# A two-layer hybrid attention and recurrent block on one core: operand splits moved to the projection, softmax scale moved behind the product, two more buffers in the mixer, three weights split ahead

## Chip, cores and metric

One core of one Trainium2 chip runs the whole program in one launch. The metric is the device time of an execution in microseconds (us), lower is better. Engines: TensorE (PE; PEld is its weight load), VectorE (DVE), ScalarE (ACT), GpSimd (POOL), and SyncE (SP), which issues all DMAs of this kernel.

## What is computed

Two layers over 1024 latent tokens and 256 context tokens of width 1024, all in float32. Only the parts around the change are shown.

```python
# layer 0: 4 differential heads (two 64-wide maps each) and 8 neighbourhood heads
w  = softmax(q0 k0) - lam * softmax(q1 k1)              # diff_attend
oa = head_rms_norm(w @ v, subln_g) * (1 - lambda_init)
s  = concat(s_loc + bias, s_ctx); p = softmax(s)        # neighbourhood_attend
ob = p_loc @ v_loc + p_ctx @ v_ctx
out = concat(oa, ob) @ w_out
# layer 1: Griffin block; both directions d, then
out = ((r_fwd + r_bwd) * gelu(y)) @ w_out
# after each mixer and each ConvFFN: x <- LN(alpha * x + gate * F(mod(x)))
```

## The kernel before, in words

**Precision.** A float32 operand of a large product is split into two fp32r tiles: `h`, a cast of the raw value, and `l = raw - h`. `split` (L101 to L103) makes the cast on ACT and the difference on DVE unless another engine is named; `weight` (L117) loads a raw weight into a ring of three (`wr`), and splits it into a ring of six (`wq`), with the difference on POOL by default. `mm3` (L122) then runs three products. In attention the split is stacked: `qs` holds `h` of a 64-wide query in partitions 0 to 63 and `l` in 64 to 127, and `kh`, `kl` hold the key's `h` and `l` in both halves.

**Order.** Each engine executes its instructions in one order. A planner lays the program out by its own costs; where `in_turn` (L91) chains instructions under a key (`att_pe`, `att_dve`, `att_act`, `att_pool`, `rnn`, `rnn_dve`), their written order is kept. SP issues loads and stores in one queue, and one that waits holds those behind it.

**Query and key projection** (`qkv`, L436 to L476). Sixteen blocks `n`, each 8 x 3 x 3 products into three PSUM chunks (banks 4, 6, 7 in rotation), copied with a scale by ACT into `q` (L463, one buffer). For the first eight blocks a rotary step follows: shuffle and two operations on DVE (L468, L469, L471), the cosine product on POOL (L470). `q` is stored to `qk_s`. Between chunks, one step of `ada` (L205) is taken: it reduces rows of the modulation weights, two DVE operations per 512 KB weight, 48 steps in all; its raw weights share the ring `wr`.

**Heads** (`heads`, L479). For each head and each half `m`, `qk_s` is loaded twice into both partition halves of `qr` and `kr`; DVE copies (L500, L503) and POOL subtracts (L501, L505; for the first head L507 on DVE) make `qs`, `kh`, `kl`. It is a generator, stepped while the head before is computed (`ahead`, L1303 and L1418).

**Attention** (`attention`, L537). 36 differential units (4 heads x (8 query blocks + context)), then 68 neighbourhood units (4 head pairs x (8 blocks x 2 heads + context)). A unit makes scores, a maximum on DVE (L1327; L1449 and L1450), an exponential on ACT, transposes on PE (L523), copies to SBUF on ACT, and the product with `v`. In a neighbourhood unit the probabilities are scaled by the reciprocal sum on DVE (L1469) before the transposes; the product has `v` (64 columns) as weights and 128 query columns streaming (L1505), so its result is already transposed and goes to `o` (L1507), stored once per pair (L1497).

**Output projection** (`proj_ln`, L680). Weight `w[k]` is loaded and split at its step `k` (L727); the planner places these.

**Recurrent mixer** (`rnn`, L1089). Eight blocks. Gate values live in lanes 0 to 3 (`lane`, L1122): lanes 0 and 1 alternate between two places from block to block, lanes 2 and 3 have one. The two scan results, in lanes 2 and 3, are added on POOL (L1178) and multiplied on DVE (L1179); all ACT functions are chained under `rnn`.

Of the kernel before, what the change touches and what calls it, by code (L numbers as in the profile page):

```python
# [57 lines left out]
class Kernel:  # L58
    def __init__(self, nc, tc, es, a):
# [4 lines left out]
        self.cast = None  # L64
        self.const = self.pool(es, "const", 1)
# [3 lines left out]
        self.qk_s = [d.tile([P, T], F32, name=f"qk_s{i}", tag=f"qk_s{i}") for i in range(16)]  # L69
# [283 lines left out]
    def qkv(self, esa):  # L353
        nc, a = self.nc, self.a
        with ExitStack() as es:
# [80 lines left out]
            with ExitStack() as es1:  # L436
# [9 lines left out]
                for n, i in enumerate((0, 4, 1, 5, 2, 6, 3, 7, 8, 12, 9, 13, 10, 14, 11, 15)):  # L446
                    w = self.weight(a["w_qk"][i])
# [10 lines left out]
                    q = qp.tile([P, T], F32, name="q", tag="q")  # L458
# [20 lines left out]
    def heads(self, n, out, sub=None):  # L479

        nc = self.nc
# [5 lines left out]
        for m in range(2):  # L487

            rows = slice(m * 64, m * 64 + 64)
            qr = pool.tile([P, T], F32, name="qr", tag="qr")  # L490
            kr = pool.tile([P, T], F32, name="kr", tag="kr")
            for t_, i in ((qr, iq), (kr, ik)):
                self.ld(t_[0:64], self.qk_s[i][rows])
                self.ld(t_[64:128], self.qk_s[i][rows])
# [4 lines left out]
            yield  # L499
            self.dve(nc.vector.tensor_copy(qs, qr))  # L500
            self.pl(nc.gpsimd.tensor_sub(qs[64:128], qr[64:128], qs[64:128].bitcast(F32)))  # L501
            yield
            self.dve(nc.vector.tensor_copy(kh, kr))  # L503
            if sub is None:
                self.pl(nc.gpsimd.tensor_sub(kl, kr, kh.bitcast(F32)))  # L505
            else:
                sub.tensor_sub(kl, kr, kh.bitcast(F32))  # L507
# [29 lines left out]
    def attention(self):  # L537
# [3 lines left out]
        with ExitStack() as es:  # L541
# [8 lines left out]
            due = []  # L550
# [36 lines left out]
            for i in range(nd, len(units) + 2):  # L587
# [92 lines left out]
    def proj_ln(self, src, w, nk, l, which, nt, x_in, x_out, nx, fold, sizes, more=(), held={},  # L680
# [8 lines left out]
        with ExitStack() as es:  # L689
# [14 lines left out]
            for size in sizes:  # L704
# [11 lines left out]
                for k in range(nk):  # L716
# [10 lines left out]
                    wh, wl = self.weight(w[k], (P, D), nc.vector)  # L727
# [361 lines left out]
    def rnn(self, left):  # L1089
# [32 lines left out]
        def lane(i, n):  # L1122

            j = {0: 0, 1: 1, 4: 2}.get(i)
            if j is not None and n % 2:
# [11 lines left out]
        def gates(n, g, xs, x, yg):  # L1137
# [39 lines left out]
            if n < KD - 1:  # L1177
                nc.gpsimd.tensor_add(ro, ro, sx[1][:, :TL])  # L1178
# [116 lines left out]
class DiffAttention:  # L1295
    def __init__(self, kn):
        self.kn = kn
        self.heads, self.outs = [], {}
        for _ in kn.heads(0, self.heads, kn.nc.vector):
            pass  # L1300
# [87 lines left out]
class NatAttention:  # L1388
# [3 lines left out]
    def __init__(self, kn, heads):  # L1392
# [4 lines left out]
        self.slot, self.pair = 0, 4  # L1397
        self.first = self.tables(0)
# [32 lines left out]
    def unit(self, pr, j, m):  # L1431
# [35 lines left out]
        for u in range(nu):  # L1467
            sl = slice(u * n // nu, (u + 1) * n // nu)
            kn.dve(nc.vector.tensor_scalar_mul(p[:, sl], p[:, sl], rr[:, u:u + 1]))  # L1469
# [8 lines left out]
        if j < NTL and nr == 9:  # L1478
            kn.turn(bb[:64, 2 * P:3 * P], p[:, 8 * GW:9 * GW])
        yield  # L1480
        for pt, g0, gn, c0 in work:
            kn.act(pT[:, g0 * P:(g0 + gn) * P], pt[:, :gn * P], AF.Copy)
        if j < NTL and nr == 9:
            kn.dve(nc.vector.tensor_copy(pT[:64, 6 * P:7 * P], bb[:64, 2 * P:3 * P]))
        yield
        if pr not in self.outs:
            self.outs[pr] = pool.tile([P, T], F32, name="o", tag="o", bufs=2)
        o = self.outs[pr]
        if j == NTL:
            for u in range(4):  # L1490
                hs, qs = slice(u % 2 * 64, u % 2 * 64 + 64), slice(u // 2 * P, u // 2 * P + P)
                for k in range(2):
                    kn.mm(ba[hs, qs], v[:, NTL + k, hs], pT[:, (2 * u + k) * P:(2 * u + k + 1) * P],
                          start=k == 0, stop=k == 1)
            yield
            kn.act(o[:, TL:], ba[:, :TC], AF.Copy)
            kn.st(kn.att_s[4 + pr], o)  # L1497
# [4 lines left out]
        hs = slice(m * 64, m * 64 + 64)  # L1502
        po = bb[hs, 3 * P:]
# [103 lines left out]
```

## Time and profile before

| what | value |
|---|---|
| median of the 3 runs shown | 3009.2 us (3004.59 to 3010.11) |
| the profiled execution's own time | 3005.08 us |
| its span, first to last instruction | 3003.3 us |
| PE / DVE / ACT / POOL busy | 95% / 69% / 49% / 31% of the span |
| granted TensorE clock, mean | 0.982 of full speed |

The span is the first to the last instruction; a busy share is an average over stages with different limits, so the stages have to be read one by one. A line of the trace names engine, source line, tiles (output <- inputs) and shapes; an idle time is put down to the instruction that released it.

### The profile page before, as it was taken

The page shows a single profiled execution, that of the slowest core. Times are in us where ns is not written, and L with a number is a line of the kernel's source. Part 1 is how long each engine was busy: PE and PEld are TensorE (multiplying, and loading weights), DVE is VectorE, ACT ScalarE, POOL GpSimd, SP SyncE. Part 2 cuts the span into 40 slices and gives each one's busy share as a digit, 9 for nine tenths or more (in the row PEclk, how much of TensorE's full clock was granted, in tenths as well). Part 3 has the DMA queues.
Part 4 walks back from the last instruction along what each step waited for, and adds up shares of the span by engine and source line. Part 5 has one row for each costly group of instructions (what it writes and reads, how often), then busy time and mean ns, then how long its engine had stood idle before and what let it go on. Part 6 is the DMA issues. An engine that isn't in the chain of part 4 may idle for free. (4 is left out here: it accounts for less than half of the span.)

```text
span 3003.3 us, 38303 instructions
## 1 busy us (share of the span) xinstructions
PE 2859.1 (95%) x14430; PEld 2367.8 (79%) x14430; DVE 2061.9 (69%) x2743; ACT 1475.3 (49%) x2358; POOL 931.3 (31%) x636
## 2 busy tenths in 40 slices
PE   8987988889999999999999999999989999999998
PEld 5876777778887888778888888777767888888876
DVE  6079759988866787875556645566688977777364
ACT  4211136666666664344444434466767554454232
POOL 4134204543300015354430000244311366761001
PEclk9998999999999999999999999999989999999999
DMA  6365542223208413632126646311146122225452
GB/s 227 128 183 194 198 158 71 71 62 87 61 29 279 175 63 107 189 119 69 69 77 215 217 158 206 100 49 50 51 164 232 64 84 79 80 77 201 146 196 99
DMA packets 133596, 381.60 MB, mean 127 GB/s; under 512 B 14334, under 2 KB 39966, under 8 KB 133282
## 3 DMA queue, kind: packets, MB, share of 16 engines
q1 hardware_dynamic: 133410, 379.15, 38.2%
q8 instruction: 113, 1.85, 0.3%
q14 instruction: 73, 0.60, 0.1%
HBM read 310.13 MB, written 68.97 MB: 126 GB/s over the span
## 5 line engine op out<-in xcount | busy, mean ns | idle before, releaser
L124 PE MATMUL pb<-wl,a 128*128 128x512 f32 x1040 | 397.6, 393 | 2.7 <-DVE wl L103 2.7
L125 PE MATMUL pb<-wh,a 128*128 128x512 f32 x1040 | 394.8, 392 | 0.8 <-DVE a L103 0.7
L123 PE MATMUL pb<-wh,a 128*128 128x512 f32 x1040 | 387.5, 393 | 7.0 <-ACT a L102 5.1
L102 ACT CAST wh<-wr 128x1024 fp32r<-128x1024 f32 x182 | 191.3, 1051 | 407.3 <-PE pb L124 282.3
L103 DVE TENSOR_TENSOR wl<-wr,wh 128x1024 fp32r<-128x1024 f32 x166 | 202.8, 1223 | 234.5 <-ACT wh L102 233.3
L123 PE MATMUL pb<-hh,wh 128*128 128x512 f32 (+1 forms) x704 | 263.8, 375 | 31.7 <-ACT q L463 31.0
L124 PE MATMUL pb<-hl,wh 128*128 128x512 f32 (+1 forms) x704 | 261.7, 372 | 1.3 <-DVE hl L669 1.3
L125 PE MATMUL pb<-hh,wl 128*128 128x512 f32 (+1 forms) x704 | 261.4, 371 | 0.0
L646 POOL TENSOR_SCALAR s<-s 128x1 f32<-128x1 f32 x36 | 16.0, 446 | 769.6 <-ACT x L645 768.9
L123 PEld LDWEIGHTS pb<-wh,a 128*128 128x128 f32 x1040 | 195.4, 188 | 50.8 <-ACT a L102 6.5
L124 PEld LDWEIGHTS pb<-wl,a 128*128 128x128 f32 x1040 | 195.3, 188 | 44.2 <-DVE wl L103 4.2
L125 PEld LDWEIGHTS pb<-wh,a 128*128 128x128 f32 x1040 | 195.3, 188 | 42.2 <-DVE a L103 2.1
L103 POOL TENSOR_TENSOR wq<-sq,wq 128x512 fp32r<-128x512 f32 x96 | 157.0, 1639 | 193.8 <-ACT wq L102 193.0
L517 ACT ACTIVATE p<-pb,nm 128x1280 f32<-128x1280 f32 (+3 forms) x160 | 158.8, 995 | 67.6 <-DVE nm L1327 65.9
L896 POOL TENSOR_TENSOR sq<-wr 128x512 f32<-128x512 f32 x72 | 120.2, 1669 | 225.4 <-DMA wr<-w_up 216.3
L123 PEld LDWEIGHTS pb<-hh,wh 128*128 128x128 f32 x704 | 137.3, 195 | 55.0 <-ACT q L463 32.7
L852 DVE SCALAR_TENSOR_TENSOR lane<-lane,cv 128x1023 f32<-128x1023 f32 x88 | 128.2, 1459 | 52.2 <-ACT lane L851 51.9
L123 PE MATMUL pb<-t,wq 128*128 128x512 f32 x400 | 157.6, 395 | 4.9 <-DVE lane L1031 4.5
L124 PE MATMUL pb<-t,wq 128*128 128x512 f32 x400 | 157.9, 395 | 0.0
L125 PE MATMUL pb<-t,wq 128*128 128x512 f32 x400 | 157.8, 395 | 0.0
L124 PEld LDWEIGHTS pb<-hl,wh 128*128 128x128 f32 x704 | 137.3, 195 | 23.8 <-DVE hl L669 1.5
L125 PEld LDWEIGHTS pb<-hh,wl 128*128 128x128 f32 x704 | 136.8, 194 | 22.6
(323 smaller groups left out, 7598.0 us busy)
## 6 DMA issues: line engine op xcount, KB each, us to landing
wr<-w_dn SPq DMA_DIRECT2D x110, 512.0 KB, 3.6
wr<-w_up SPq DMA_DIRECT2D x88, 512.0 KB, 3.6
wr<-ada_w SPq DMA_DIRECT2D x80, 512.0 KB, 3.9
ar<-g_s SPq DMA_DIRECT2D x88, 256.0 KB, 3.7
wr<-w_ao SPq DMA_DIRECT2D x32, 512.0 KB, 5.4
g_s<-lane SPq DMA_DIRECT2D x22, 640.0 KB, 3.0
x_s<-y SPq DMA_DIRECT2D x26, 512.0 KB, 6.0
x<-x_s SPq DMA_DIRECT2D x26, 512.0 KB, 5.5
```

What stands on the lines that cost most here:

```text
L102: self.cast = self.nc.scalar.copy(h, raw)
L103: (sub or self.nc.vector).tensor_sub(l, raw, h.bitcast(F32))
L123: i = mm(out, a[0], b[0], start=first, stop=False, **kw)
L124: mm(out, a[0], b[1], start=False, stop=False, **kw)
L125: j = mm(out, a[1], b[0], start=False, stop=last, **kw)
L517: self.in_turn("att_act", self.nc.scalar.activation(*args, **kw))
L646: nc.gpsimd.tensor_scalar(rs, sq, 1.0 / D, EPS, op0=ALU.mult, op1=ALU.add)
L852: nc.vector.scalar_tensor_tensor(c[:, 1:], u[:, :n - 1], cvw[:, 0:1], c[:, 1:], op0=ALU.mult, op1=ALU.add)
L896: op(have[n], x, y)
```

## The change

Seven edits.

1. In the q/k projection the weight's difference goes from POOL to DVE, and the rotary cosine product too. `q` gets a second buffer. Each block is then split: a cast `h` on ACT, `l` on DVE in place of `q`, and both are stored (two stores for one).
2. `heads` loads `h` and `l` straight into `qs`, `kh`, `kl`: six loads per half for four, no DVE and no POOL work.
3. A neighbourhood unit no longer scales its probabilities (L1469 goes). Its product takes the transposed probabilities as weights (128 columns) and streams 64 columns of `v`; the reciprocal sum becomes the scale of ACT's copy to `o`.
4. `o` is therefore untransposed: 40 blocks of 128 x 128 are turned on PE and copied by ACT, one at a time with later units (`turned`), the rest at the end (`finish`).
5. `weight_ahead`: the first three weights of the output projection are loaded and split in the attention's own order, in the last five units.
6. In the mixer lanes 2 and 3 of odd blocks get tiles of their own.
7. The sum of the two scans goes from POOL to DVE (blocks 0 to 6).

```diff
-        self.qk_s = [d.tile([P, T], F32, name=f"qk_s{i}", tag=f"qk_s{i}") for i in range(16)]
+        self.qk_s = [d.tile([2, P, T], F32, name=f"qk_s{i}", tag=f"qk_s{i}") for i in range(16)]
...
-                    w = self.weight(a["w_qk"][i])
+                    w = self.weight(a["w_qk"][i], sub=nc.vector)
...
-                    q = qp.tile([P, T], F32, name="q", tag="q")
+                    q = qp.tile([P, T], F32, name="q", tag="q", bufs=2)
+                    h = qp.tile([P, T], F32R, name="qh", tag="qh")
...
-                        nc.gpsimd.tensor_mul(q[:, :TL], q[:, :TL], cos)
+                        nc.vector.tensor_mul(q[:, :TL], q[:, :TL], cos)
                         nc.vector.tensor_add(q[:, :TL], q[:, :TL], rot)
-                    self.st(self.qk_s[i], q)
+                    self.split(q, h, q.bitcast(F32R))
+                    self.st(self.qk_s[i][0], h.bitcast(F32))
+                    self.st(self.qk_s[i][1], q)
...
-            qr = pool.tile([P, T], F32, name="qr", tag="qr")
-            kr = pool.tile([P, T], F32, name="kr", tag="kr")
-            for t_, i in ((qr, iq), (kr, ik)):
-                self.ld(t_[0:64], self.qk_s[i][rows])
-                self.ld(t_[64:128], self.qk_s[i][rows])
...
-            self.dve(nc.vector.tensor_copy(qs, qr))
-            self.pl(nc.gpsimd.tensor_sub(qs[64:128], qr[64:128], qs[64:128].bitcast(F32)))
...
+            for half in range(2):
+                to = slice(half * 64, half * 64 + 64)
+                self.ld(qs[to].bitcast(F32), self.qk_s[iq][half, rows])
+                self.ld(kh[to].bitcast(F32), self.qk_s[ik][0, rows])
+                self.ld(kl[to].bitcast(F32), self.qk_s[ik][1, rows])
+                yield
...
+                if 0 <= i - len(units) + 5 < 3:
+                    self.weight_ahead(i - len(units) + 5)
...
+            n.finish()
+    def weight_ahead(self, k):
+        raw = self.ring.tile([P, D], F32, name="wr", tag="wr", bufs=3)
+        h, l = (self.ring.tile([P, D], F32R, name="w" + i, tag="wq", bufs=6) for i in "hl")
+        self.ld(raw, self.a["w_ao"][k])
+        self.act(h, raw, AF.Copy)
+        self.dve(self.nc.vector.tensor_sub(l, raw, h.bitcast(F32)))
+        self.ahead[k] = h, l
...
-                    wh, wl = self.weight(w[k], (P, D), nc.vector)
+                    wh, wl = self.ahead.pop(k, None) or self.weight(w[k], (P, D), nc.vector)
...
-            if j is not None and n % 2:
+            if j is None and n % 2:
+                return big(f"lane{i}")
+            if n % 2:
...
-                nc.gpsimd.tensor_add(ro, ro, sx[1][:, :TL])
+                nc.vector.tensor_add(ro, ro, sx[1][:, :TL])
...
-            kn.dve(nc.vector.tensor_scalar_mul(p[:, sl], p[:, sl], rr[:, u:u + 1]))
...
+        out = self.turned(bb, self.unit_no) if j < NTL else None
+        self.unit_no += 1
...
+        if out:
+            out()
...
-        po = bb[hs, 3 * P:]
+        po = ba[:, :GW]
         for k, (s, n, tb) in enumerate(seq):
-            kn.mm(po, v[:n, tb, hs], pT[:n, s * P:(s + 1) * P], start=k == 0, stop=k == len(seq) - 1)
+            kn.mm(po, pT[:n, s * P:(s + 1) * P], v[:n, tb, hs], start=k == 0, stop=k == len(seq) - 1)
         yield
-        kn.act(o[hs, j * P:(j + 1) * P], po, AF.Copy)
+        kn.act(o[:, j, hs], po, AF.Copy, scale=rr)
+        if m == 1:
+            self.due.append((self.unit_no, pr, j))
+    def turned(self, bank, now):
+        if self.before or not self.due or self.due[0][0] > now:
+            return None
+        kn, (_, pr, t) = self.kn, self.due.pop(0)
+        kn.turn(bank[:, 3 * P:], self.outs[pr][:, t])
+        if t == 0:
+            self.st = self.pool.tile([P, T], F32, name="st", tag="st", bufs=1)
+        def move():
+            kn.act(self.st[:, t * P:(t + 1) * P], bank[:, 3 * P:], AF.Copy)
+            if t == NT - 1:
+                kn.st(kn.att_s[4 + pr], self.st)
+        return move
+    def finish(self):
+        bank = itertools.cycle((6, 7))
+        while self.due:
+            self.turned(self.kn.banks(next(bank)), self.unit_no)()
```

The context unit of a pair changes in the same way (four products of 64 columns each, four scaled copies).

## Rows read from the trace of the kernel before

**Rows 1.** Busy time by stage: stretch in us from the span's start, its length, then busy us of each engine with the number of instructions, granted TensorE clock, DMA share, GB/s. The stretches are: q/k projection; differential attention; neighbourhood attention; recurrent mixer.

```profile
155.00:425.00 270.00, 235.50 (x1162) 199.68 (x1162) 200.22 (x243) 46.23 (x72) 75.75 (x24) 0.94 0.55 177
425.00:690.00 265.00, 230.39 (x1588) 204.57 (x1586) 239.50 (x330) 173.06 (x381) 120.66 (x138) 0.97 0.30 86
690.00:905.00 215.00, 211.81 (x1591) 179.52 (x1590) 160.15 (x406) 138.59 (x341) 53.71 (x35) 1.00 0.22 64
...
1925.00:2190.00 265.00, 248.69 (x1176) 204.85 (x1174) 169.90 (x166) 177.49 (x160) 101.03 (x40) 0.97 0.16 51
```

**Rows 2.** The same view for the two parts of the q/k projection.

```profile
164.00:300.00 136.00, 109.32 (x528) 92.17 (x527) 128.06 (x145) 20.52 (x34) 57.81 (x18) 0.91 0.62 191
300.00:425.00 125.00, 117.18 (x591) 99.79 (x590) 72.15 (x99) 22.54 (x37) 17.93 (x7) 0.97 0.48 160
```

**Rows 3.** Who waited for whom in 155 to 425 us: total us, times, longest us.

```profile
PE pb L123 <- ACT q L463: 31.0, 8, 6.8
...
ACT q L463 <- DMA qk_s<-q: 84.1, 10, 16.3
...
SPq L83 <- DVE wr L205: 148.1, 41, 13.0
```

**Rows 4.** Groups of instructions in 155 to 425 us: line, engine, operation, shapes, count, then busy us and mean ns of one, then idle before.

```profile
L205 DVE SCALAR_TENSOR_TENSOR pb<-wr,c_rows 128x1024 f32<-128x1024 f32 x48 | 78.5, 1636 | 108.5 <-ACT c_rows L192 90.9 <-DMA wr<-ada_w 17.5
L205 DVE SCALAR_TENSOR_TENSOR wr<-wr,c_rows 128x1024 f32<-128x1024 f32 x48 | 67.1, 1399 | 1.6 <-issue 0.4
...
L468 DVE STREAM_SHUFFLE rot<-q 128x1024 f32<-128x1024 f32 x8 | 11.0, 1370 | 0.0
...
L103 POOL TENSOR_TENSOR wl<-wr,wh 128x1024 fp32r<-128x1024 f32 x14 | 42.0, 3002 | 100.5 <-ACT wh L102 94.5 <-DVE pb L205 3.4 <-PE pb L125 2.6
L470 POOL TENSOR_TENSOR q<-q,cos 128x1024 f32<-128x1024 f32 x8 | 26.3, 3289 | 86.3 <-DVE rot L468 86.3
```

**Rows 5.** Single lines in the same stretch: count, shortest, median and longest duration in ns, first and last start in us.

```profile
L205 DVE SCALAR_TENSOR_TENSOR pb<-wr,c_rows x48: 1221/1230/3978, 164.7 to 421.7; 128x1024 f32<-128x1024 f32 x48
...
L469 DVE TENSOR_TENSOR rot<-rot,sin x8: 1214/3386/3404, 171.6 to 298.7; 128x1024 f32<-128x1024 f32 x8
```

**Rows 6.** DVE in order of time in one differential head (485 to 545 us): start us, duration us.

```profile
491.56 0.22 DVE L1339 SCALAR_TENSOR_TENSOR cf<-ss,nlam,rr 128x1 f32<-128x1 f32 x1
...
508.97 0.22 DVE L1339 SCALAR_TENSOR_TENSOR cf<-ss,nlam,rr 128x1 f32<-128x1 f32 x1
...
515.96 2.91 DVE L1339 SCALAR_TENSOR_TENSOR cf<-ss,nlam,rr 128x1 f32<-128x1 f32 x1
...
539.52 0.22 DVE L1339 SCALAR_TENSOR_TENSOR cf<-ss,nlam,rr 128x1 f32<-128x1 f32 x1
```

**Rows 7.** Groups in 425 to 690 us, columns as in rows 4.

```profile
L500 DVE CAST qs<-qr 128x1280 fp32r<-128x1280 f32 x9 | 7.3, 816 | 0.0
...
L505 POOL TENSOR_TENSOR kl<-kr,kh 128x1280 fp32r<-128x1280 f32 x9 | 26.3, 2918 | 17.3 <-DVE rr L1338 15.8 <-DVE kh L503 1.5
```

**Rows 8.** All engines in order of time around 436 us; in brackets the idle time before and its releaser.

```profile
436.36 1.04 ACT L102 CAST wh<-wr 128x1024 fp32r<-128x1024 f32 x1 [5.30 <-DMA wr<-w_ao]
...
437.96 4.13 PE L520 MATMUL pb<-v,wT 128*128 128x128 f32 x20 [4.87 <-ACT wT L517]
```

**Rows 9.** Groups in 690 to 905 us, columns as in rows 4.

```profile
L1469 DVE TENSOR_SCALAR p<-p,rr 128x832 f32<-128x832 f32 x29 | 27.9, 962 | 1.0
...
L517 ACT ACTIVATE o<-pb 64x128 f32<-64x128 f32 x60 | 16.3, 272 | 59.1 <-PE pb L520 59.0
...
L520 PE MATMUL pb<-wT,v 128*64 128x128 f32 x772 | 94.2, 277 | 2.2 <-DVE wT L1484 2.2
```

**Rows 10.** PE alone in order of time in the neighbourhood stage: start us, time from the first start to the last end. A float32 product is two instructions; `128*64` is the weights' shape, `128x128` the streaming operand's.

```profile
765.60 0.40 PE L520 MATMUL pb<-kl,qs 128*128 128x512 f32 x1
765.83 0.28 PE L520 MATMUL pb<-kh,qs 128*128 128x256 f32 x1
765.95 0.28 PE L520 MATMUL pb<-kl,qs 128*128 128x256 f32 x1
766.07 0.92 PE L523 MATMUL pb<-ident,p 128*128 128x128 f32 x7
766.92 1.88 PE L520 MATMUL pb<-wT,v 128*64 128x128 f32 x14
```

**Rows 11.** The same view in a differential unit: weights of 128 columns.

```profile
563.52 2.40 PE L520 MATMUL pb<-v,wT 128*128 128x128 f32 x20
```

**Rows 12.** PE in order of time at 14 us: a product that streams only 2 columns against weights of 128 columns (5 partitions), columns as in rows 10.

```profile
13.81 1.05 PE L232 MATMUL pb<-sel,ada_rows 5*128 5x2 f32 x8 [0.66 <-ACT ada_rows L229]
```

**Rows 13.** Who waited for whom in the mixer, 1900 to 2190 us, columns as in rows 3.

```profile
PE pb L123 <- ACT lane L1120: 13.0, 6, 2.7
...
ACT lane L1120 <- DVE lane L1179: 25.4, 6, 4.8
```

**Rows 14.** All engines in order of time in one block of the mixer, as in rows 8.

```profile
2056.46 2.40 POOL L1178 TENSOR_TENSOR lane<-lane 128x1024 f32<-128x1024 f32 x1 [5.70 <-DVE lane L1174]
...
2060.22 1.33 ACT L1120 ACTIVATE lane<-pb,cv 128x1280 f32<-128x1280 f32 x1 [4.74 <-DVE lane L1179]
2061.60 0.50 PE L123 MATMUL pb<-xh,wg 128*128 128x512 f32 x1 [2.67 <-ACT lane L1120]
```

**Rows 15.** The issue of the modulation weights' loads: KB each, median us from issue to landing.

```profile
wr<-ada_w SPq DMA_DIRECT2D x80, 512.0 KB, 3.9
```

More of the change, by code (lines that the diff above doesn't have):

```diff
@@ L64, in __init__ @@
         self.cast = None
+        self.ahead = {}
         self.const = self.pool(es, "const", 1)
@@ L476, in qkv, with heads @@
             self.fold(0, 0, 0, 0, 3, 4)
-    def heads(self, n, out, sub=None):
-        nc = self.nc
+    def heads(self, n, out):
         pool = self.sets[n % 2]
@@ L549, in attention @@
             steps = [self.first] + [o.unit(*u) for o, *u in units[1:]]
-            due = []
+            due = n.before = []
             def s(i, n=1):
@@ L1298, in __init__ @@
         self.heads, self.outs = [], {}
-        for _ in kn.heads(0, self.heads, kn.nc.vector):
+        for _ in kn.heads(0, self.heads):
             pass
@@ L1397, in __init__ @@
         self.slot, self.pair = 0, 4
+        self.due, self.unit_no, self.st = [], 0, None
         self.first = self.tables(0)
@@ L1466, in unit @@
         kn.dve(nc.vector.reciprocal(rr, ss))
-        for u in range(nu):
-            sl = slice(u * n // nu, (u + 1) * n // nu)
-            kn.dve(nc.vector.tensor_scalar_mul(p[:, sl], p[:, sl], rr[:, u:u + 1]))
         yield
@@ L1486, in unit @@
         if pr not in self.outs:
-            self.outs[pr] = pool.tile([P, T], F32, name="o", tag="o", bufs=2)
+            self.outs[pr] = pool.tile([P, NT, P], F32, name="o", tag="o", bufs=2)
         o = self.outs[pr]
@@ L1490, in unit @@
             for u in range(4):
-                hs, qs = slice(u % 2 * 64, u % 2 * 64 + 64), slice(u // 2 * P, u // 2 * P + P)
                 for k in range(2):
-                    kn.mm(ba[hs, qs], v[:, NTL + k, hs], pT[:, (2 * u + k) * P:(2 * u + k + 1) * P],
-                          start=k == 0, stop=k == 1)
+                    kn.mm(ba[:, u * GW:(u + 1) * GW], pT[:, (2 * u + k) * P:(2 * u + k + 1) * P],
+                          v[:, NTL + k, u % 2 * GW:(u % 2 + 1) * GW], start=k == 0, stop=k == 1)
             yield
-            kn.act(o[:, TL:], ba[:, :TC], AF.Copy)
-            kn.st(kn.att_s[4 + pr], o)
+            for u in range(4):
+                kn.act(o[:, NTL + u // 2, u % 2 * GW:(u % 2 + 1) * GW], ba[:, u * GW:(u + 1) * GW],
+                       AF.Copy, scale=rr[:, u:u + 1])
+            self.due += [(self.unit_no, pr, t) for t in range(NTL, NT)]
             return
@@ L1501, in unit @@
             seq.append((6, 64, r0 // 2 + 4))
-        hs = slice(m * 64, m * 64 + 64)
-        po = bb[hs, 3 * P:]
+        hs = slice(m * GW, m * GW + GW)
+        po = ba[:, :GW]
         for k, (s, n, tb) in enumerate(seq):
-            kn.mm(po, v[:n, tb, hs], pT[:n, s * P:(s + 1) * P], start=k == 0, stop=k == len(seq) - 1)
+            kn.mm(po, pT[:n, s * P:(s + 1) * P], v[:n, tb, hs], start=k == 0, stop=k == len(seq) - 1)
         yield
-        kn.act(o[hs, j * P:(j + 1) * P], po, AF.Copy)
+        kn.act(o[:, j, hs], po, AF.Copy, scale=rr)
[17 more added lines that the diff above has]
+            self.turned(self.kn.banks(next(bank)), self.unit_no)()
 def _blocks(w, n):
```

7 lines of the change are left out of this document (removed).

## The prediction

> **What bounds the kernel now.** I read the busy time by stage first [rows 1]. TensorE does the work that sets the end: it is busy 235.5 of 270 us in the q/k projection, 230.4 of 265 in the differential attention, 211.8 of 215 in the neighbourhood attention and 248.7 of 265 in the mixer. So three of the four stages that the change touches have TensorE idle time to win (34.5, 34.6 and 16.3 us), and the neighbourhood stage has 3.2. In the first two the granted clock is 0.94 and 0.97, so there are also stretches at 1.2 GHz in place of 2.4, after TensorE has stood still.
>
> Second, the waits, to see who keeps TensorE waiting. In the q/k projection it waits 31.0 us for the scaled copy L463, and that copy waits 84.1 us for the store of the one buffer `q`; SP's loads wait 148.1 us for VectorE's modulation steps [rows 3]. VectorE is 94% busy in the first part (128.1 of 136 us), and 58% in the second [rows 2]. Third, VectorE's groups, against the shortest duration of the same instruction: L205 takes 1.64 us on average and 1.22 at its shortest, L469 2.58 (its median 3.39) and 1.21 [rows 4, 5]. The long ones are as long as the GpSimd operations of 3.0 and 3.3 us beside them [rows 4]: VectorE is held while GpSimd reads. The same appears in the differential units: L1339, a column of one element, takes 0.22 us, and 2.91 while GpSimd makes `kl` (2.92 us) [rows 6, 7].
>
> **Part 1, q/k projection.** Removed from GpSimd: 16 weight differences of 3.00 us and 8 cosine products of 3.29. Added on VectorE: the same 24 at 1.21 us (the shortest L469, same shape), and 16 differences of 1280 columns at 1.21 x 1.25 = 1.5 us. Removed there: the first head's copies. Nothing of this stage is left on GpSimd, so every VectorE operation goes at its shortest. A block with a rotary step and three modulation steps then costs VectorE 3 x 2 x 1.22 = 7.3, and 0.7 for reading the sums, plus shuffle 1.37 and three products or sums 3.6, plus 1.2 and 1.5: 15.7 us. Today such blocks follow each other in (298.7 - 171.6) / 7 = 18.2 us (first and last start of L469) [rows 5]. At the same 94% of VectorE they take 16.7: -10 us over 7 intervals. The eight blocks without a rotary step need 10.7 us of VectorE; TensorE needs 24 x (0.23 + 0.23 + 0.12) = 13.9 us for a block [rows 10]. They take (425 - 299) / 8 = 15.8 us today; with two `q` buffers the copy no longer waits for a store one block old. I take 14.3 for them, since the new ACT cast and the store of the single `qh` are still in line: -12 us. Sum of the part: **-22 us**. Covers: 16 casts of 1.3 us are 21 us more on ACT, which is busy 46 of 270 us; without that cover they would delay L463. Sixteen more stores of 640 KB stand in SP's queue, whose waits for VectorE get shorter; with DMA at 0.55 of its time [rows 1] there is room, and if there were none, the next thing late would be the modulation weights. Bounds: -45 (all of TensorE's idle time and the clock) and +18 (VectorE's added 3.9 us in eight blocks with nothing won, less the 13 us of the first head's copies).
>
> Here a rule speaks against the change. The Trainium skill, Perfetto Trace Analysis, Optimizing Scalar/DVE Operations, says that with a saturated VectorE some work may be moved off to ScalarE or even GpSimd, and warns that the two share an SBUF read port, so that it may not help. The first half by itself forbids this move in a stretch with VectorE at 94%, and would give +18 in place of -22; the rows side with the warning.
>
> **Part 2, heads.** Four differential heads each prepare the next head in four of their units. Units without that work follow in (508.97 - 491.56) / 3 = 5.80 us, the four with it in (539.52 - 508.97) / 4 = 7.64 [rows 6]. The difference holds a copy of 0.81 us [rows 7] and one blocked operation. Both go; loads into `qs`, `kh`, `kl` (6 per half for 4) stand in SP's queue after the release of the head before last, with DMA at 0.30. 4 x 4 x 1.84 = **-29 us**. TensorE's 34.6 us of idle time and the clock bound it at -37; copies alone, 16 x 0.81, at -13. In the neighbourhood stage the same removal is worth nothing, since TensorE is 98% busy there. If the cover of the loads were gone, the next head's scores would be late.
>
> **Part 3, weights ahead.** One load of an output weight was placed at the start of the attention: ACT sat 5.30 us before its cast, and TensorE 4.87 before the next product [rows 8]. In the attention's order this cast cannot stand there: **-5 us** (bounds -6 and 0). The three casts and differences now stand among the last units, where ACT waits 59 us for TensorE [rows 9]: nothing; if a weight landed late, the exponentials behind the cast would be late.
>
> **Part 4, the neighbourhood product.** L1469 goes (27.9 us in its larger group [rows 9]), from an engine that waits for TensorE: nothing. The product's two instructions stream 64 columns for 128, but against weights of 128 columns for 64. Today's take (1.88 - 0.28) / 13 = 0.12 us apart [rows 10]; weights of 128 columns with 128 streaming take (2.40 - 0.28) / 19 = 0.112 [rows 11], and with only 2 streaming (1.05 - 0.25) / 7 = 0.114 [rows 12]. So the load of 128 columns sets the spacing, and the shorter stream gains nothing: 0. Forty transposes are new, at (0.92 - 0.27) / 6 = 0.11 us: 4.4 us, and as many copies of some 0.3 us on ACT, hidden by the 59 us. A transpose waits for an ACT copy one unit older; I add 0.1 us for each start, and take off the 2.2 us that TensorE waits for L1484, since VectorE has less ahead of it: **+5 us**. Bounds: -50 (the stream sets the spacing: 896 instructions x 0.056) and +15. The last transposes, copies and the store come 7 weights ahead of their use: nothing.
>
> **Part 5, the mixer.** The sigmoid into lane 2 waits for L1179 of the block before, which waits for GpSimd's sum of 2.40 us; ACT sits 4.74 us and TensorE 2.67 [rows 14]: 25.4 and 13.0 us in six blocks [rows 13]. With a second lane the sigmoid waits for its own product only. I count the 13.0 us and 2 for the clock (0.97 in this stretch): **-15 us**. The sum on VectorE costs 7 x 1.2 us, hidden: VectorE is busy 170 of 265. Bounds -20 and -4 (a new wait of ACT takes the place).
>
> **Sum.** -22 - 29 - 5 + 5 - 15 = -66 us against the profiled execution's 3005.1: 2939. The median of the runs shown is 4 us above that execution, so I forecast a median of **2943 us**. A measurement here tells about 0.2%, 6 us, from no change.
>
> **Rivals.** (a) The q/k projection gives nothing: VectorE stays the bound with the added work in full, +18 in place of -22. For it: VectorE's 94%. Against: nothing stays on GpSimd to hold it. Time: 2943 + 40 = 2983.
> (b) The stream, not the weight load, sets the spacing: -50 for +5, time 2888. For it: 512 and 256 columns are 0.23 and 0.12 us apart [rows 10]. Against: rows 12. The Trainium skill, TensorE: Matmul & The Clock Gate, Back-to-back issue gap, gives columns / 2.4 + 2.5 ns for an isolated product, which would halve it; the same page, LDWEIGHTS, gives weight columns / 1.2, 107 ns for 128 columns. Rows 12 agree with the second.
> (c) Slower. In the q/k projection the weight's difference now stands in VectorE's queue between modulation steps, and those wait for loads in SP's queue behind two stores. If TensorE waits at each of 15 blocks for one step (2.65 us) and one landing (3.9 us [rows 15]), part 1 is +98 and the time 3063. From 44 / 15 = 2.9 us a block on the change is no gain. Against: the ring holds three weights, so a difference has a block's time.
> (d) The change does less than it says: the mixer's wait only moves to another lane, and the planner's early cast finds another stall: parts 3 and 5 at nothing, 2963.
>
> **How the numbers follow.** Chances: forecast 0.66, (a) 0.12, (d) 0.08, (b) 0.04, (c) 0.07, and 0.03 for (a) with parts 4 and 5 at their worse bounds, which ends within 0.2%. Forecast, (a), (b) and (d) are faster: 0.90; slower 0.07. The forecast's own range is 2920 to 2968. To hold 8 in 10 the range goes up to (a): 2918 to 2984; (b) and (c) are left out.
>
> **What would show it.** Right: VectorE's L205 and L469 at 1.2 us throughout; the copy L463 no longer waiting for a store; all differential units about 5.8 us apart; no wait of ACT for L1179; the neighbourhood stage longer by a few us. Wrong: TensorE waiting for a weight's difference on VectorE, or for the cast of `qh`, in the q/k projection; the neighbourhood product at half its spacing; the q/k projection as long as before.

## The result, and the profile after

The changed kernel takes **2925.9 us** (median of 4 runs, 2924.45 to 2927.53), the kernel before 3009.5 beside it: ratio 0.9726, 95% interval 0.9709 to 0.9743. Further on, a time is followed in brackets by such a ratio to the kernel before, run beside it, and its interval. The profiled span fell from 3003.3 to 2922.6 us. A second series gave 2925.05 against 3007.91, ratio 0.9730 (0.9713 to 0.9747).

Stage lengths are read between events that both kernels have: the first scaled copy of `q`, the first coefficient `cf` of a differential unit, the first maximum `mx` of a neighbourhood unit, the first product of the output projection, the first store of the first feed-forward, the first scan and the last store of the mixer, the first store of the second feed-forward, and the end. So a projection's row reaches into the feed-forward behind it, and the first feed-forward's row into the start of the mixer. In us of the profiled executions:

| stage | before | after | difference | predicted |
|---|---|---|---|---|
| q/k projection | 258.3 | 222.9 | -35.4 | -22 |
| differential attention | 247.9 | 208.6 | -39.3 | -29 and -5 |
| neighbourhood attention | 225.0 | 221.8 | -3.2 | +5 |
| output projection | 205.6 | 207.7 | +2.1 | 0 |
| first feed-forward, two halves | 883.4 | 886.2 | +2.8 | 0 |
| mixer | 259.2 | 240.3 | -18.9 | -15 |
| mixer's output projection | 132.6 | 140.4 | +7.8 | 0 |
| second feed-forward, two halves | 634.2 | 638.4 | +4.2 | 0 |

Up to the mixer's end 97 us are won and 5 lost. Behind it 12 us are given back. The prediction had none of these 17 us.

Busy time by stage after the change; columns as in [rows 1]. The stretches: q/k projection, differential, neighbourhood, mixer, and 85 us around the mixer's last store (2143.8 us).

```profile
155.00:390.00 235.00, 224.97 (x1162) 192.29 (x1160) 193.98 (x275) 65.38 (x87) 0.00 (x0) 0.99 0.74 245
390.00:598.00 208.00, 201.38 (x1467) 184.72 (x1466) 181.80 (x277) 161.64 (x356) 66.18 (x121) 0.99 0.55 134
598.00:815.00 217.00, 210.97 (x1673) 201.80 (x1672) 107.60 (x346) 152.22 (x401) 21.54 (x24) 0.98 0.33 83
...
1850.00:2090.00 240.00, 237.56 (x1152) 197.14 (x1151) 183.87 (x173) 170.79 (x152) 87.23 (x34) 0.99 0.17 55
2090.00:2175.00 85.00, 71.48 (x274) 54.76 (x273) 66.84 (x71) 48.97 (x52) 9.32 (x4) 0.88 0.50 172
```

TensorE is idle for 10.0 us in the first stretch, where it was 34.5; its clock rose from 0.94 to 0.99, and GpSimd has nothing left there. In the second, 34.6 us of idle time became 6.6, in the mixer 16.3 became 2.4. In the last stretch TensorE is idle for 13.5 us at a clock of 0.88; the same stretch of the kernel before (2182.6 to 2267.6 us) has 11.4 us and 0.90. The loss lies behind the store: in the next 86 us TensorE is idle for 8.0 us, 0.8 before.

The q/k projection after: waits in 155 to 390 us, which answer to [rows 3].

```profile
ACT q L465 <- DMA qk_s<-q: 34.9, 5, 9.1
...
PE pb L124 <- ACT q L465: 0.9, 1, 0.9
...
SPq L84 <- DVE wr L206: 96.8, 41, 12.8
```

TensorE's wait for the copy fell from 31.0 to 0.9 us, the copy's wait for stores from 84.1 to 34.9. VectorE's groups in that stretch, and the sine product alone (shortest, median, longest in ns; first and last start), which answer to [rows 4, 5]:

```profile
L206 DVE SCALAR_TENSOR_TENSOR pb<-wr,c_rows 128x1024 f32<-128x1024 f32 x48 | 59.4, 1237 | 65.3 <-ACT c_rows L193 54.5 <-DMA wr<-ada_w 10.7
...
L104 DVE TENSOR_TENSOR q<-q,qh 128x1280 fp32r<-128x1280 f32 x16 | 23.9, 1494 | 3.2 <-ACT qh L103 3.2
L104 DVE TENSOR_TENSOR wl<-wr,wh 128x1024 fp32r<-128x1024 f32 x14 | 17.2, 1229 | 4.1 <-ACT wh L103 4.1
```

```profile
L471 DVE TENSOR_TENSOR rot<-rot,sin x8: 1206/1228/1285, 170.4 to 277.3; 128x1024 f32<-128x1024 f32 x8
```

Every operation goes at about its shortest, as predicted: L206 1.24 us (1.64 before), the sine product's median 1.23 (3.39).

A differential head after: the coefficient in order of time, which answers to [rows 6].

```profile
495.57 0.22 DVE L1349 SCALAR_TENSOR_TENSOR cf<-ss,nlam,rr 128x1 f32<-128x1 f32 x1
500.94 0.22 DVE L1349 SCALAR_TENSOR_TENSOR cf<-ss,nlam,rr 128x1 f32<-128x1 f32 x1
506.59 0.22 DVE L1349 SCALAR_TENSOR_TENSOR cf<-ss,nlam,rr 128x1 f32<-128x1 f32 x1
512.74 0.22 DVE L1349 SCALAR_TENSOR_TENSOR cf<-ss,nlam,rr 128x1 f32<-128x1 f32 x1
```

The coefficient takes 0.22 us in each, and these units stand 5.4, 5.7 and 6.2 us apart. No ScalarE wait for the mixer's product (25.4 us in [rows 13]) is left in the mixer's waits.

### The profile page after: what moved, and what is told of

It reads as the page before. It is cut to its first block, busy times and chain, and to the rows that moved or that the text cites. A ratio compares the mean times of both kernels' runs of the same rounds, so it can differ in the third digit from the quotient of the medians.

```text
span 2922.6 us, 38331 instructions
## 1 busy us (share of the span) xinstructions
PE 2830.8 (97%) x14470; PEld 2373.8 (81%) x14470; DVE 1972.4 (67%) x2676; ACT 1505.0 (51%) x2426; POOL 751.7 (26%) x575
## 3 DMA queue, kind: packets, MB, share of 16 engines
q8 instruction: 113, 1.85, 0.3%
## 4 chain that ended last, share of the span: by engine, by line
PE 74%; DVE 10%; issue 3%; ACT 3%; DMA 3%; POOL 1%; DVEq 0%; SPq 0%; ACTq 0%; POOLq 0%
PE pb L125 20%; PE pb L126 20%; PE pb L124 20%; PE pb L516 9%; PE pb L519 3%; DVE wr L206 1%; DVE pb L206 1%; DMA wr<-ada_w 1%; DVE nm L1337 1%; DVE y L826 1%; DVE wl L104 1%; DVE y L651 0%; POOL sq L904 0%; DVE lane L862 0%; DVE p L1354 0%
## 5 line engine op out<-in xcount | busy, mean ns | idle before, releaser
L104 DVE TENSOR_TENSOR wl<-wr,wh 128x1024 fp32r<-128x1024 f32 x179 | 218.5, 1222 | 278.1 <-ACT wh L103 276.0
L124 PE MATMUL pb<-hh,wh 128*128 128x512 f32 (+1 forms) x704 | 256.8, 365 | 6.3 <-ACT wh L103 4.7
L516 PE MATMUL pb<-v,wT 128*128 128x64 f32 (+2 forms) x1568 | 194.6, 275 | 0.9 <-ACT st L513 0.8
L516 PEld LDWEIGHTS pb<-v,wT 128*128 128x128 f32 (+1 forms) x1568 | 186.8, 193 | 3.8 <-ACT st L513 1.1
L513 ACT ACTIVATE p<-pb,nm 128x1280 f32<-128x1280 f32 (+3 forms) x160 | 159.2, 999 | 34.9 <-DVE nm L1337 33.9
```

What stands on the lines that cost most here:

```text
L104: (sub or self.nc.vector).tensor_sub(l, raw, h.bitcast(F32))
L124: i = mm(out, a[0], b[0], start=first, stop=False, **kw)
L513: self.in_turn("att_act", self.nc.scalar.activation(*args, **kw))
L516: self.in_turn("att_pe", self.nc.tensor.matmul(*args, **kw))
```

## The experiments

**Placement of the mixer's lane, engine of its sum, and a repeat.** Four runs told where the mixer's gain comes from and why the work behind it got slower.

`after_again` is the changed kernel once more: 

> The changed kernel once more, on the chip of the three runs that follow, as their common base. Every theory expects 2926 us within 3.

Measured: 2925.05 us; its stages agree with the first profile within 3.5 us each.

`lanes_even`:

```diff
-            if j is None and n % 2:
+            if j is None and n % 2 == 0:
                 return big(f"lane{i}")
-            if n % 2:
+            if j is not None and n % 2:
```

> Lanes 2 and 3 get their own tiles in the even blocks of the mixer instead of the odd ones, so that the last block (an odd one) has its lanes outside the mixer's pool. Theory M1: the 8 us that the changed kernel gives back behind the mixer come from the loads of gate, norm vectors and x, which reuse the pool's space and so wait for the last block's product. Then they go out some 10 to 20 us before that product, TensorE no longer waits 3.6 us for y L826, the time is 2918 to 2921, and the mixer itself keeps its gain (no wait of ACT for the product of the block before). Rival M2: the loss there is VectorE's or SP's order and not the space: 2926 within 2.

Measured: **2913.99 us** (0.9693, 0.9677 to 0.9709), 11 us less than the changed kernel beside it; M1 held in direction, but had 2918 to 2921. The mixer is as long (240.8), the mixer's projection 131.8 us, where the changed kernel has 140.4 and the kernel before 132.6; the second feed-forward got 1.0 us shorter. What differs is in SP's queue around the mixer's end. First the kernel before, then the changed kernel, then `lanes_even`: start, duration, what is issued.

```profile
2222.27 0.43 SPq L83 DMA_DIRECT2D g<-gate_s  x1
...
2236.43 0.32 SPq L88 DMA_DIRECT2D r_s<-lane  x1
```

```profile
2143.79 0.33 SPq L89 DMA_DIRECT2D r_s<-lane  x1
2144.17 0.43 SPq L84 DMA_DIRECT2D g<-gate_s  x1
2144.65 1.59 SPq L84 DMA_DIRECT2D in<-lnv  x2
2146.28 3.03 SPq L84 DMA_DIRECT2D x<-x_s  x4
```

```profile
2128.58 0.43 SPq L84 DMA_DIRECT2D g<-gate_s  x1
2129.06 1.05 SPq L84 DMA_DIRECT2D in<-lnv  x2
2130.15 1.42 SPq L84 DMA_DIRECT2D x<-x_s  x3
...
2142.74 0.32 SPq L89 DMA_DIRECT2D r_s<-lane  x1
```

In the kernel before, the gate's load went out 14.2 us ahead of the mixer's last store; in the changed kernel it comes 0.4 us after it, and with the lane in the even blocks 14.2 us ahead again. The last block has an odd number: in the changed kernel it writes the new lane, and the next stage's loads go out only behind that lane's store. That the tiles' place is the cause is what the run shows, since it changes nothing else. A part of the price shows as a wait of the changed kernel, in 2144 to 2230 us (one wait, seen by the weight load and by the product):

```profile
PEld pb L124 <- DVE y L826: 4.1, 1, 4.1
...
PE pb L124 <- DVE y L826: 3.6, 1, 3.6
```

`lanes_even` has no such wait: in the 86 us behind its store TensorE is idle for 1.4 us, for 8.0 in the changed kernel. Why the second feed-forward is still 3.3 us longer than before, and the first 2.8, is not shown.

`mix_add_gpsimd` puts the sum back:

```diff
-                nc.vector.tensor_add(ro, ro, sx[1][:, :TL])
+                nc.gpsimd.tensor_add(ro, ro, sx[1][:, :TL])
```

> Only the sum of the two scans goes back to GpSimd; the second lanes stay. Theory M3: the second lane alone takes the wait away, since the sigmoid then waits for a product two blocks old; the sum's engine is worth nothing: 2926 within 3, no wait of ACT for the product. Rival M4: the sum on GpSimd (2.4 us, and the wait before the product) is still on the path: 2932 to 2940.

Measured: 2926.59 us, mixer 240.0. The sum's engine is worth nothing once there are two lanes.

`mix_one_lane` takes the second lane away and leaves the sum on VectorE:

```diff
-            if j is None and n % 2:
-                return big(f"lane{i}")
-            if n % 2:
+            if j is not None and n % 2:
```

> Only the second lanes are taken back; the sum stays on VectorE. Theory M3: the wait stays, shorter by the 2.5 us that the product waited for GpSimd in each block: ACT waits 1.5 to 2.5 us in place of 4.7 in six blocks, TensorE 0 to 1 in place of 2.7; the mixer gives back 3 to 8 us of its 19, but the loads behind it go out early again (8 us): 2920 to 2928. Rival M4: with the sum on VectorE the wait is gone altogether, and the lanes were not needed: 2916 to 2919.

Measured: 2925.66 us. Its mixer waits again (1850 to 2105 us):

```profile
ACT lane L1128 <- DVE lane L1187: 19.3, 6, 3.5
...
PE pb L124 <- ACT lane L1128: 7.2, 5, 1.5
```

The mixer takes 250.0 us, 9.7 more than with the lane, the projection behind it 133.8, 6.6 less, and the second feed-forward 3.5 less: the total is the same. M3's total held, but its waits are too short (3.2 us for ScalarE and 1.4 for TensorE at a time), and it had at most 8 us for the 9.7. The sum's move by itself, without the lane, has taken the mixer from 259.2 to 250.0 us: sum and lane take away the same wait, the lane all of it. So the second lane as it was put in wins nothing in all; its place took back what it won.

**The q/k projection.** `qk_gpsimd` undoes the move between engines:

```diff
-                    w = self.weight(a["w_qk"][i], sub=nc.vector)
+                    w = self.weight(a["w_qk"][i])
...
-                        nc.vector.tensor_mul(q[:, :TL], q[:, :TL], cos)
+                        nc.gpsimd.tensor_mul(q[:, :TL], q[:, :TL], cos)
```

> The changed kernel with the weight's difference and the cosine product of the q/k projection back on GpSimd; the two q buffers, the split and the two stores stay. Theory Q1: VectorE held by GpSimd's reads was what kept the projection slow: L206 and the sine product grow to means of 1.4 to 2.5 us again, the stage goes from 223 us to 243 to 255, and the kernel to 2945 to 2957. Rival Q2: the second q buffer, which lets ACT's scaled copy go on without the store, made the gain: the stage stays within 223 to 230, and the kernel within 2925 to 2932.

Measured: 2942.17 us (0.9795, 0.9774 to 0.9817), stage 237.3, 14.4 longer: between the two theories (Q1 had 243 to 255, Q2 up to 230). VectorE's steps are long again:

```profile
L206 DVE SCALAR_TENSOR_TENSOR pb<-wr,c_rows 128x1024 f32<-128x1024 f32 x46 | 74.2, 1612 | 107.7 <-ACT c_rows L193 92.4 <-DMA wr<-ada_w 15.3
```

`q_one_buffer` has a single `q` again, everything else as changed:

```diff
-                    q = qp.tile([P, T], F32, name="q", tag="q", bufs=2)
+                    q = qp.tile([P, T], F32, name="q", tag="q")
```

> The changed kernel with one q buffer in place of two; nothing else. Theory Q1: the store of q now comes later than before (behind the split), but VectorE is free, so ACT waits for it: 5 to 12 us of the stage come back, 2930 to 2937. Rival Q2: the buffer is the main part: the stage returns to 245 us or more, 2947 to 2965.

Measured: 2964.38 us (0.9863, 0.9845 to 0.9881), stage **260.0**, as long as before the change. Waits and VectorE's step in 155 to 415 us:

```profile
ACT q L465 <- DMA qk_s<-q: 69.7, 13, 9.5
...
PE pb L124 <- ACT q L465: 31.4, 8, 8.4
```

```profile
L206 DVE SCALAR_TENSOR_TENSOR pb<-wr,c_rows 128x1024 f32<-128x1024 f32 x44 | 54.3, 1235 | 73.0 <-PE pb L126 53.8 <-DMA wr<-ada_w 19.0
```

VectorE is unhindered (1.24 us) and yet nothing is won: the copy waits for the one buffer's store, and TensorE 31.4 us for the copy, as before (31.0). The two parts hang together: without the second buffer the move wins nothing, without the move the buffer wins 21 of 35 us. (The split stays in this run, so the one buffer is also held longer than before the change.)

**The neighbourhood product.** `stream_128` streams both heads' 128 columns and keeps 64; `nat_old` has the old product, with the scaling on VectorE.

```diff
...
-            kn.mm(po, pT[:n, s * P:(s + 1) * P], v[:n, tb, hs], start=k == 0, stop=k == len(seq) - 1)
+            kn.mm(po, pT[:n, s * P:(s + 1) * P], v[:n, tb], start=k == 0, stop=k == len(seq) - 1)
...
```

```diff
...
-        for k, (s, n, tb) in enumerate(seq):
-            kn.mm(po, pT[:n, s * P:(s + 1) * P], v[:n, tb, hs], start=k == 0, stop=k == len(seq) - 1)
+            kn.mm(po, v[:n, tb, hs], pT[:n, s * P:(s + 1) * P], start=k == 0, stop=k == len(seq) - 1)
...
-        kn.act(o[:, j, hs], po, AF.Copy, scale=rr)
+        kn.act(o[hs, j * P:(j + 1) * P], po, AF.Copy)
...
```

> The neighbourhood product streams all 128 columns of v (both heads of the pair) against the same 128-column weights, and ACT copies only the head's 64 of the result. Theory N1: the load of the 128 columns sets the spacing (0.112 us), so twice the stream costs nothing: the neighbourhood stage stays at 222 us within 3, the kernel at 2925 within 4. Rival N2: the stream sets it, at half a microsecond per 512 columns and two passes: 0.05 us more for each of some 860 instructions, so 30 to 45 us more, 2955 to 2970.

> The changed kernel with the neighbourhood units as they were: probabilities scaled on VectorE, product with v as the weights, result stored without turning. Theory N1: TensorE bounds this stage either way, the forty transposes (4.4 us) are saved, and VectorE's scaling is hidden: the stage goes from 222 to 218 to 222, the kernel to 2921 to 2925. Rival N3: with the scaling off VectorE, TensorE's small waits were what fell: the stage returns to 225 or more, the kernel to 2928 to 2933.

Measured: 2929.39 us (0.9746, 0.9728 to 0.9764), stage 222.2; and 2923.8 us (0.9728, 0.9706 to 0.9751), stage 222.8. Neither differs from the changed kernel (221.8) by more than two profiles of it differ (221.8, 225.3). TensorE alone in order of time, columns as in [rows 10]: the changed kernel, `stream_128`, `nat_old`.

```profile
642.21 0.82 PE L519 MATMUL pb<-ident,p 128*128 128x128 f32 x6
642.87 1.45 PE L516 MATMUL pb<-v,wT 128*128 128x64 f32 x12
644.13 0.48 PE L516 MATMUL pb<-kh,qs 128*128 128x512 f32 x1
```

```profile
643.15 0.82 PE L519 MATMUL pb<-ident,p 128*128 128x128 f32 x6
643.81 1.50 PE L516 MATMUL pb<-v,wT 128*128 128x128 f32 x12
645.07 0.48 PE L516 MATMUL pb<-kh,qs 128*128 128x512 f32 x1
```

```profile
639.81 0.82 PE L519 MATMUL pb<-ident,p 128*128 128x128 f32 x6
640.55 1.52 PE L516 MATMUL pb<-wT,v 128*64 128x128 f32 x12
642.01 0.50 PE L516 MATMUL pb<-kh,qs 128*128 128x512 f32 x1
```

Twelve instructions and the step to the next product take 1.26 us with 64 streaming columns and 1.26 with 128: the stream does not set the spacing, as predicted; over all such units the steps between the instructions have a median of 0.112 us in both. The other units have two instructions more, on a block of 64 rows, and there the stream shows: fourteen instructions take 1.74 us, and 1.85 with 128 columns (medians of 32 units, so 3.5 us in all by estimate), a small part of N2's price. The old form takes 1.46 in the rows, and its six transposes with the step to the product 0.74 in place of 0.66. Over the stage the median from the last transpose to the first product is 0.20 us in `nat_old` and 0.11 in the changed kernel; for fourteen instructions the old form takes 1.81.

The stage is as long in `nat_old` because two things cancel: TensorE is busy for 220.0 us in it and for 214.9 in the changed kernel's, but idle for 2.7 and 6.9. And the output projection, into which the last units and transposes reach, falls from 207.7 to 205.4 us in `nat_old`, as before the change (205.6). Both stages together take 429.5 us in the changed kernel (433.0 in its repeat) and 428.2 in `nat_old`.

**The heads.** `heads_gpsimd` puts one GpSimd subtraction back into each of the 16 steps, `heads_copies` one VectorE copy, both into a buffer that nobody reads.

```diff
...
+                qr = pool.tile([P, T], F32, name="qr", tag="qr")
+                self.pl(self.nc.gpsimd.tensor_sub(qr[to], kh[to].bitcast(F32), kl[to].bitcast(F32)))
...
```

```diff
...
+                qr = pool.tile([P, T], F32, name="qr", tag="qr")
+                self.dve(self.nc.vector.tensor_copy(qr[to], kh[to].bitcast(F32)))
...
```

> The changed kernel with GpSimd back in the preparation of the heads, and nothing else of the old preparation: in each of the four steps of a head one GpSimd subtraction of 64 x 1280 elements from the loaded parts into a buffer that nobody reads; no copy on VectorE. It is extra work and not needed for the output. Theory H1 (GpSimd holds VectorE, and a one-element operation of VectorE in the chain of the unit waits for it: this is what the 1.84 us per unit were): units with a step grow from 5.4-6.1 us by about 1 us and more, the stage of the differential attention goes from 208 to 222-235 us, L1349 or L1339 have some of nearly the length of the GpSimd operation, total 2938-2955. Rival H2 (the copy of 1280 columns in VectorE's queue was the cost, or the loads through the scratch of both halves): no longer than 211 us, total within 5 us of the changed kernel.

> The changed kernel with one VectorE copy of 64 x 1280 elements put back into each of the four steps of a head, into a buffer that nobody reads, and nothing on GpSimd; extra work, not needed for the output. H1: a copy of about 0.4-0.8 us is hidden in most units; the stage of 208 us grows by at most 16 x 0.4 = 6 us, total 2926-2932. H2: units with a step grow by the copy and more, 16 x 0.8 to 1.84 = 13 to 29 us, total 2939-2955.

Measured: 2937.71 us (0.9772, 0.9747 to 0.9797), stage 216.7, and 2930.37 us (0.9748, 0.9728 to 0.9769), stage 210.1. So in the stage the subtractions cost 8.1 us and the copies 1.5, where the old preparation cost 29 and more. The copies are hidden, as H1 said; the subtractions lie between the two theories. The changed kernel, then `heads_gpsimd`, in 380 to 600 us:

```profile
L1354 DVE SCALAR_TENSOR_TENSOR p<-p,cf 128x512 f32<-128x512 f32 (+1 forms) x72 | 61.9, 860 | 0.0
```

```profile
L1367 DVE SCALAR_TENSOR_TENSOR p<-p,cf 128x512 f32<-128x512 f32 (+1 forms) x70 | 81.4, 1163 | 0.0
...
L1362 DVE SCALAR_TENSOR_TENSOR cf<-ss,nlam,rr 128x1 f32<-128x1 f32 (+1 forms) x36 | 10.7, 297 | 1.2
```

```profile
L496 POOL TENSOR_TENSOR qr<-kh,kl 64x1280 f32<-64x1280 f32 x16 | 48.5, 3028 | 0.7
```

VectorE is held, but at another operation: L1367, the product that uses the coefficient, takes 1.16 us where the changed kernel has 0.86, the coefficient 0.30. The order of time shows why. In the kernel before, GpSimd's operation starts with the coefficient, which stands at 515.96 us and lasts 2.91 us in [rows 6]; so it is, within 0.13 us, at 15 of the 16 steps, and at 8 of them the coefficient takes 2.9 us:

```profile
515.93 2.92 POOL L505 TENSOR_TENSOR kl<-kr,kh 128x1280 fp32r<-128x1280 f32 x1 [1.99 <-DVE rr L1338]
```

In `heads_gpsimd` it starts 2.2 us behind the coefficient (2.1 to 2.7 at 15 of the 16 steps):

```profile
512.27 3.18 POOL L496 TENSOR_TENSOR qr<-kh,kl 64x1280 f32<-64x1280 f32 x1
```

```profile
510.11 0.22 DVE L1362 SCALAR_TENSOR_TENSOR cf<-ss,nlam,rr 128x1 f32<-128x1 f32 x1
```

Operations of 2.9 to 3.2 us on GpSimd are there in both, and they lengthen VectorE's work by nearly as much: coefficient and product together take 70 us in the stage of the changed kernel, 92 in `heads_gpsimd` and 100 in the kernel before. What they delay differs. In 400 to 600 us of `heads_gpsimd` TensorE waits 0.6 us for that product and 8.5 for the head's output `o` (L1396); in 442 to 662 us of the kernel before it waits 7.2 us for the product, 9.1 for `o` (L1373) and 6.5 for another copy of ScalarE (`st`). That the start on the chain is what made up the rest of the 29 us is read from these orders and waits; it is not shown, since no run shifted the start alone, and copy and subtraction together were not run.

**Weights ahead.** `no_weight_ahead` leaves the split among the last units out:

```diff
-                if 0 <= i - len(units) + 5 < 3:
+                if False:
```

> The changed kernel without the casts and differences of the first three output weights among the last attention units (the planner issues them again as before). Theory W1 (as predicted: one cast was placed at the attention's start and held ScalarE for 5.3 us and TensorE for 4.9): the stall is back, total 5 us longer, 2929-2932. Rival W2 (with the shorter stages the planner places the cast elsewhere or its load lands in time): no stall, total within 3 us of the changed kernel, and TensorE has a wait of a few us at the start of the output projection or none.

Measured: **2940.91 us** (0.9782, 0.9759 to 0.9804): 15 more than the changed kernel: W1's stall, at three times its size. ScalarE and TensorE at the attention's start:

```profile
414.53 1.04 ACT L103 CAST wh<-wr 128x1024 fp32r<-128x1024 f32 x1 [13.85 <-DMA wr<-w_ao]
```

```profile
417.15 1.11 PE L519 MATMUL pb<-ident,p 128*128 128x128 f32 x4 [13.47 <-DVE o L1383]
```

The cast of [rows 8] is back, and waits 13.85 us for its load, not 5.30. The load was issued at 401.2 us among those of the heads, with the DMA engines at 90% and more in every slice from 390 to 423 us. The changed kernel issues the same three loads at the same place (398.1 to 402.9 us), and there no engine waits for them, since their casts stand behind, at 802 us and later.

**The lane's better place with a third buffer.** `best` is `lanes_even` and

```diff
-                    q = qp.tile([P, T], F32, name="q", tag="q", bufs=2)
+                    q = qp.tile([P, T], F32, name="q", tag="q", bufs=3)
```

> The changed kernel with the mixer's new lane in the blocks of even number, as in the run before that put it there, and a third buffer for q in the q/k projection, since ScalarE still waits 34.9 us for stores of q there. If the store of q still sets a part of the stage (theory Q2), the stage of 223 us gets 3-10 us shorter: total 2905-2911. If what is left are the modulation's loads and the first weights (VectorE's steps waiting for ada_w and the copy waiting for TensorE), the stage stays: total 2912-2916.

Measured: 2917.56 us (0.9705, 0.9683 to 0.9727), q/k stage 224.5 (222.9 with two buffers). A third buffer wins nothing (1.6 us more than the expectation had for that case), though ScalarE still waited 34.9 us for stores with two: that wait isn't TensorE's. The time does not differ from that of `lanes_even`; the better place of the lane is what beats both kernels.

## Why the prediction was right, step by step

The forecast was 2943 us, and 2926 came out, inside the range. The direction held, and so did the mechanisms of parts 1, 2, 3 and 5 in the main. The sum was partly lucky: the stages of the five parts gave -97 us where the terms add to -66, and 17 us were lost in stages that the prediction put at nothing. Without these losses the time would have been some 2909 us, below the range.

**Part 1** was mis-sized: -35 for -22. From the first to the last sine product it takes 106.9 us, not 127.1: -20 for -10, blocks 15.3 us apart and not the 16.7 predicted. The step that failed was the 15.7 us of VectorE's work for such a block, which added up durations. In order of time in one block after the change:

```profile
201.53 1.22 DVE L471 TENSOR_TENSOR rot<-rot,sin 128x1024 f32<-128x1024 f32 x1
202.66 1.22 DVE L472 TENSOR_TENSOR q<-q,cos 128x1024 f32<-128x1024 f32 x1
203.80 1.22 DVE L206 SCALAR_TENSOR_TENSOR wr<-wr,c_rows 128x1024 f32<-128x1024 f32 x1
204.94 0.08 DVE L206 DVE_READ_ACCUMULATOR wr<-wr,c_rows 128x1 f32 x1
204.94 1.23 DVE L206 SCALAR_TENSOR_TENSOR pb<-wr,c_rows 128x1024 f32<-128x1024 f32 x1
```

Operations of 1.22 us start 1.14 us apart, and the reading of a sum lies beside the next one. So a block has 99.2 / 7 = 14.2 us of VectorE (its busy time from 170 to 277 us), and at the 93% that it is busy there (99.2 / 107) that gives the 15.3. From the last sine product to the first coefficient -15 against -12. The prediction put the first gain down to VectorE alone and the buffer into the second; `q_one_buffer` shows the buffer is needed in the whole stage, and keeping GpSimd's operations off VectorE, by `qk_gpsimd`, is worth 14. Its sign that the copy no longer waits for a store did not come: 34.9 us of such waits are left, but TensorE waits only 0.9 us for the copy. Rival (a), VectorE as the bound with the added work in full, did not come: the stage lost 35 us with that work on VectorE. The rule on moving work off a saturated VectorE, in the Trainium skill's page Perfetto Trace Analysis, Optimizing Scalar/DVE Operations, would have kept the 24 operations on GpSimd; here that costs 14 us, and the page's warning beside it is what the trace bears out.

**Part 2** was right in size: the five intervals between coefficients that hold the second head's preparation sum to 36.7 us before and 29.4 after, 7.3 a head, where 4 x 1.84 was charged (10.1, 7.3, 5.4 and 7.4 in the four heads). Its ascription (a copy of 0.81 us and one blocked operation) is only half shown: copies alone cost 1.5 us, GpSimd alone 8, and the rest of the 29 is open.

**Part 3** was right for the kernel before (the coefficient's second interval fell from 11.8 to 5.5 us, -6.3 for -5), but its worth in the changed kernel is 15 us. The prediction costed the stall as it stood; it did not ask where ScalarE would stand when the load was issued. In the kernel before, the load went out at 425.8 us and its cast began 10.6 us later; ScalarE had other work until 431.1. In `no_weight_ahead` the cast began 13.3 us after the issue, not much more, but ScalarE's work ended at 400.7, before the issue, so it stood for all of it.

**Part 4** is too small to be told from nothing: the kernel's ratio is 0.9728 in `nat_old` and 0.9726 or 0.9730 with the change. (Its terms as given, 4.4 and 40 x 0.1 less 2.2, add to 6.) The stage's -3 against +5 does not show a wrong sign: with the old product put back the stage is 222.8 us, so 2.2 of the 3.2 come from elsewhere, and with the output projection, whose +2 the prediction put at nothing, the change costs 1.3 us by the first profile and 4.8 by the repeat. The stream gains nothing of size, as said, so rival (b) did not come, and a turned tile costs its 0.11 us (2.02 against 1.91 us from the transposes to the next scores, medians with and without one). The missing term is the change of weight shape: from the transposes to the next scores the old form takes 2.20 us in the rows above and the new one 1.92. Most of it is taken back (TensorE is idle for 4.2 us more in the stage) where ScalarE waits for the store of the one turned tile, and TensorE for the copy of `o` queued behind. In 598 to 815 us of the changed kernel:

```profile
ACT st L513 <- DMA att_s<-st: 5.8, 3, 3.2
...
PE pb L519 <- ACT o L513: 4.2, 5, 2.3
```

**Part 5** was right: -19 for -15. TensorE's idle time went from 16.3 to 2.4 us, and the clock rose from 0.97 to 0.99. That the sum's move is hidden also held. Rival (d) held in one way that it did not name: the wait did not go to another lane, but the room of the new lane delayed the next stage's loads. The step that fell short is "With a second lane the sigmoid waits for its own product only": the prediction asked who waits for the lane inside the mixer, and not what its space is used for next.

**Rival (c)**, weight differences queueing behind modulation steps, cost TensorE nothing of size: it waits 4.7 us for `wh` and 1.5 for `wl` in the stage.

## What to carry to other kernels

A buffer that wins its wait can lose it at the stage's end: look up whose space the last iteration holds, and choose the parity so that the last one doesn't hold it. Two remedies for one stage (here a freed engine and a second buffer) are not a sum of their parts; cost them together and undo them one at a time. A blocked operation costs what the chain behind it waits for, so look at where it starts as well as at how long it is.

## What was not expected of the hardware

Between products with weights of 128 columns, a product with weights of 64 columns costs some 0.09 us at its start (0.20 against 0.11 us from the last transpose) and up to 0.2 us by the next product (1.46 against 1.26 for twelve instructions; 1.81 against 1.74 for fourteen, where both forms have a block of 64 rows at the end). VectorE starts its next operation before the last one's time is over (1.14 us apart at 1.22 us each). A load of 512 KB, issued while the DMA engines were 90% busy, released its cast 13.3 us after its issue began (401.2 to 414.5 us; the issue alone took 4.1), where the median to landing, over the 8 of that weight's 32 loads whose landing is recorded, is 3.6 us.
